# Three more column pairs of the up projection in the form with 42 products, with the buffers that this takes

## The chip, the cores and the metric

The kernel runs on one core of one Trainium2 chip. The metric is the device time of one execution in microseconds (us). The time before is 1391.71 us, the median of 3 runs (1391.12 to 1394.36). The profiled execution took 1392.02 us, and its span from the first to the last instruction is 1390.1 us.

## The reference, cut to what matters

One decoder layer over 256 tokens, all in float32. A mixing part (two branches, a gated delta rule and block attention) takes about half of the time and is not touched. What is touched is the first matmul of the MLP, `h @ w_up`:

```python
h = rms_norm(x, ln2[l])                                     # 256 x 2048
u = causal_dwconv(h @ w_up[l], ffn_conv[l], ffn_conv_bias[l])   # w_up: 2048 x 11264
u_gate, u_val = jnp.split(u, 2, axis=-1)                    # 5632 each
x = x + (jax.nn.silu(u_gate) * u_val) @ w_down[l]
```

## The kernel before

**Precision.** TensorE multiplies in fp32r. Each float32 operand is therefore split into a high part, `wh`, which is a cast on ScalarE (`split`, L104 and L105), and a low part, `wl`, which is the rest, a subtraction on VectorE (`low`, L101 and L102). A product of two operands is three matmuls: high by high, high by low, low by high. I call one such matmul of 128x512 a product step, or just a product, as the title counts them; 48 and 42 are numbers of these matmuls.

**Tiling.** The up projection is cut into 11 column pairs, `c` = 0 to 10 (loop at L1102). A pair has two sides of 512 columns each, side 0 for the gate and side 1 for the value, and two halves of 128 tokens, so four PSUM banks. D_MODEL is cut into 16 K-blocks of 128 rows. One fetch (`fetch`, L115) brings four K-blocks of one side, a quarter, as four DMAs of 256 KB each, issued on the POOL queue, into a buffer `wraw` of which there are four in rotation. A quarter has two raw halves; each is split once and then used by 12 matmuls, so a quarter takes 24 matmuls and a pair 8 x 24 = 192. `wh` and `wl` are rings of four slots: the cast for a part waits until TensorE has used up the part four places earlier.

**The shorter form.** For `c` in `UPS` (L30; before: 1 to 6) the first quarters of both sides are done together by `fewer` (L1028). The host interleaves their rows so that the four raw halves `r10`, `r11`, `r20`, `r21` are the four blocks of a 2x2 by 2x2 block product, done with seven block products for eight. That is 42 matmuls for 48, and it costs additions on VectorE: three before the first products (`t1 = r10 + r11`, `r11 += r21`, `t2 = t1 + r21`, all 128x1024), a fourth later (`t2 += r20`), four on PSUM banks (128x512), two copies on ScalarE, and seven splits where the two quarters need four. Six of the seven block products come first, then side 0's other three quarters (72 matmuls), then the function `rest` adds two banks and does the seventh block product with `r21`, then side 1's other three quarters.

**Buffers of the shorter form.** The first raw block `(r10, r11)` is an ordinary fetch. The second, `(r20, r21)`, is fetched during the pair before (L1113) into rows of `acts` that hold no results yet, `spare(28, 8)`. `acts` (44 rows of 256 columns) takes the activations; pair `c` fills rows 4c to 4c+3. `t1` is `acts` rows 24 to 27, `t2` rows 36 to 39, the fold sums rows 40 to 43. So the form could not be used for pairs whose results fill those rows. The weights fetched ahead into `acts` do not use up a `wraw` buffer.

**Order.** The program is written in the order of the loops; a scheduler then orders the instructions of each engine. Behind the matmuls run generators (`bg`), advanced once every 8 matmuls or so (`main_mm`, L93) except while `paused` is set, which `fewer` does: the convolutions of the results (`convolved`, L968; per side one 128x1024 transpose `xt<-ut` and eight or twelve short VectorE operations) and the transposition of the residual (`residual_turned`, L953; four transposes `xt<-x`, each followed by 16 small DMAs). A finished side is moved from PSUM into `ut` (L1082), of which there are two buffers.

## Time and profile before

| | |
|---|---|
| median of 3 runs | 1391.71 us (1391.12 to 1394.36) |
| the profiled execution | 1392.02 us |
| its span | 1390.1 us |
| granted TensorE clock | 0.999 |
| TensorE matmuls busy | 1378.3 us, 7186 matmuls |
| VectorE busy | 1096.4 us |
| ScalarE busy | 815.6 us |
| up projection, first to last matmul | 696.6 to 1157.3 us |
| its matmuls | 2076 |

The rows are from one profiled execution. The span lies inside the execution's own time; 1.9 us lie around it, and the median of the runs is 0.3 us under that time. Engines are PE (TensorE), DVE (VectorE), ACT (ScalarE), POOL (GpSimd, here a DMA queue). In a row of the timeline stand the start, the duration, the engine, the line, the operation, out<-in, the shape, the count, and in brackets the idle time before it with what ended it. A matmul's duration of 0.38 us overlaps with the next one's, so its cost in a stream is the distance between two starts.

### The profile page before, as it was taken

Reading aid. Unit: us, or ns where it says so; the run is one execution under the profiler, and the core shown is the slowest. Engines: PE = TensorE matmul, PEld = TensorE weight load, DVE = VectorE, ACT = ScalarE, POOL = GpSimd, SP = SyncE. Lnnn points to the kernel's source line nnn. Section 1 sums busy time; section 2 is a strip of 40 time slices with the busy share of each in tenths; the row PEclk is TensorE's granted clock in tenths of the full one; section 3 lists DMA queues with packets and bytes.
Section 4 is the critical chain, followed back from the end, with each engine's and each line's share of the span. In section 5 each row is a group of like instructions: output and inputs, shape, how many; then the busy total and the mean of one; then the engine's idle time right before and its main releaser. Section 6 shows DMA issues by size and latency. Waiting matters only on the chain.

```text
span 1390.1 us, 20248 instructions
## 1 busy us (share of the span) xinstructions
PE 1378.3 (99%) x7186; PEld 1194.9 (86%) x7186; DVE 1096.4 (79%) x1616; ACT 815.6 (59%) x1023; POOL 244.8 (18%) x424
## 2 busy tenths in 40 slices
PE   9999999999999999999999999999999999999997
PEld 8998899888888888889988888888888888888886
DVE  7988886977665446777668999999876777999995
ACT  6766545645466544445556676676665566676763
POOL 0021000200001100001344434434444320000000
PEclk9999999999999999999999999999999999999999
DMA  9566653567545565686567889898898976656561
GB/s 369 180 207 221 211 203 130 170 205 277 184 145 203 198 209 191 206 277 252 189 190 222 229 233 236 209 254 217 244 235 223 240 218 232 233 192 237 179 245 66
DMA packets 220165, 297.46 MB, mean 214 GB/s; under 512 B 171320, under 2 KB 173760, under 8 KB 198816
## 3 DMA queue, kind: packets, MB, share of 16 engines
q1 hardware_dynamic: 171984, 196.45, 44.3%
q0 software_dynamic: 30240, 96.04, 22.0%
q10 hardware_dynamic: 17840, 3.67, 1.4%
q8 instruction: 56, 0.92, 0.3%
q14 instruction: 45, 0.37, 0.1%
HBM read 273.48 MB, written 3.15 MB: 199 GB/s over the span
## 4 chain that ended last, share of the span: by engine, by line
PE 93%; DMA 4%; DVE 2%; SPq 1%; issue 0%; ACT 0%; DVEq 0%
PE ps_up L94 33%; PE pd L94 16%; PE ps_gate L94 12%; PE ps_gdn L94 9%; PE ps_wo L94 6%; PE ps_br L94 6%; PE ps_v L94 3%; PE ps_z L94 3%; PE ps_moba L94 2%; DMA wraw<-in_w_moba 2%; SPq L481 1%; DVE wl L102 1%; DMA xv<-xv 1%; PE ps_gdn L268 1%; DMA xs<-in_xw 0%; DMA dT<-X 0%
## 5 line engine op out<-in xcount | busy, mean ns | idle before, releaser
L102 DVE TENSOR_TENSOR wl<-wraw,wh 128x1024 fp32r<-128x1024 f32 (+1 forms) x464 | 557.9, 1211 | 208.1 <-ACT wh L105 204.8
L105 ACT CAST wh<-wraw 128x1024 fp32r<-128x1024 f32 (+1 forms) x464 | 477.6, 1038 | 411.2 <-PE ps_up L94 103.2
L94 PE MATMUL ps_up<-wh,h 128*128 128x512 f32 x1288 | 378.8, 380 | 0.2 <-DVE x L924 0.2
L94 PEld LDWEIGHTS ps_up<-wh,h 128*128 128x128 f32 x1288 | 241.5, 188 | 42.2 <-issue 0.6
L94 PE MATMUL ps_up<-wl,h 128*128 128x512 f32 x644 | 237.9, 381 | 1.2 <-DVE wl L102 1.0
L120 POOL DMA_DIRECT2D wraw<-in_w_up x328 | 174.5, 538 | 250.7 <-DVE wl L102 241.4
L94 PE MATMUL ps_gate<-wh,hc 128*128 128x512 f32 x512 | 155.4, 382 | 0.0
L94 PEld LDWEIGHTS ps_up<-wl,h 128*128 128x128 f32 x644 | 120.9, 188 | 24.3 <-DVE wl L102 3.7
L94 PE MATMUL ps_gdn<-hc,wh 128*128 128x256 f32 x720 | 124.2, 276 | 0.0
L94 PEld LDWEIGHTS ps_gate<-wh,hc 128*128 128x128 f32 x512 | 95.8, 188 | 16.3
L94 PEld LDWEIGHTS ps_gdn<-hc,wh 128*128 128x128 f32 x720 | 108.4, 188 | 1.3 <-issue 0.6
L94 PE MATMUL ps_gate<-wl,hc 128*128 128x512 f32 x256 | 98.0, 383 | 0.0
L94 PE MATMUL ps_gdn<-hc,wl 128*128 128x256 f32 x360 | 97.9, 275 | 0.0
L94 PE MATMUL ps_wo<-mc,wh 128*128 128x512 f32 x256 | 85.6, 379 | 0.0
L94 PE MATMUL pd<-tt,ah 128*128 128x512 f32 x282 | 82.0, 380 | 0.0
L94 PE MATMUL ps_moba<-wh,hc 128*128 128x512 f32 x256 | 77.1, 381 | 0.0
L94 PE MATMUL ps_wo<-mc,wl 128*128 128x256 f32 x256 | 70.5, 276 | 0.0
L105 ACT CAST tt<-wraw 128x1024 fp32r<-128x1024 f32 x46 | 47.1, 1044 | 36.3 <-PE pd L94 24.7
L94 PEld LDWEIGHTS ps_gdn<-hc,wl 128*128 128x128 f32 x360 | 67.1, 188 | 0.3
L94 PEld LDWEIGHTS pd<-tt,ah 128*128 128x128 f32 x282 | 52.9, 188 | 9.1
L94 PE MATMUL pd<-wh,ah 128*128 128x512 f32 x156 | 59.1, 380 | 0.0
L94 PE MATMUL pd<-wl,ah 128*128 128x512 f32 x156 | 59.1, 380 | 0.0
(465 smaller groups left out, 2177.1 us busy)
## 6 DMA issues: line engine op xcount, KB each, us to landing
wraw<-in_w_up POOLq DMA_DIRECT2D x328, 256.0 KB, 4.6
wraw<-in_w_dn SPq DMA_DIRECT2D x44, 1024.0 KB, 6.5
wraw<-in_w_gate SPq DMA_DIRECT2D x32, 1024.0 KB, 5.0
wraw<-in_w_gdn SPq DMA_DIRECT2D x22, 1024.0 KB, 4.9
wraw<-in_w_moba SPq DMA_DIRECT2D x16, 1024.0 KB, 6.2
wraw<-in_w_o SPq DMA_DIRECT2D x16, 1024.0 KB, 5.4
uc<-xt SPq DMA_DIRECT2D x352, 32.0 KB, 5.1
wraw<-in_w_z SPq DMA_DIRECT2D x8, 1024.0 KB, 6.9
```

The source lines that it names most:

```text
L94: r = pe.matmul(ps, a, b, start=start, stop=stop, skip_group_check=True)
L102: return (eng or dve).tensor_tensor(lo, src, hi.bitcast(F32), op=ALU.subtract)
L105: casts.append(act.copy(hi, src))
L120: fetcher[0].dma_start(raw[:, 512 * q:512 * q + 512], src[q])
L268: pe.matmul(ps_q0[:, b], wq[:, j, b * P:(b + 1) * P], xs[:, j], start=(j == b == 0), stop=False, skip_group_check=True)
L481: eng.dma_start(dst[32 * e:32 * e + 32, :, 32 * a:32 * a + 32], xt[32 * a:32 * a + 32, :, 32 * e:32 * e + 32])
```

## The change

`UPS` becomes 1 to 9, so that pairs 7, 8 and 9 take the shorter form too; the host's layout and the ring's first slot follow from `UPS`. The buffers are moved to make room. The fold sums get tiles of their own (`fold`, `fold2`), paid for with the second buffer of `ut`. The second raw block goes to `acts` rows 32 to 39, `t2` to rows 40 to 43, `t1` to rows 28 to 31. In pairs 8 and 9 rows 28 to 31 are taken, so `t1` is written over `r10`, and for that `r10` is split before the additions. In pair 9, the tenth, rows 32 to 39 are taken too, so its second raw block is fetched into an ordinary `wraw` buffer when the pair begins.

```diff
-UPS = (1, 2, 3, 4, 5, 6)
+UPS = (1, 2, 3, 4, 5, 6, 7, 8, 9)
...
-    def fewer(ps, raw1, raw2):
+    def fewer(c, ps, raw1, raw2):
         c11, c12, c21, c22 = ps
-        fold_v, fold_y = spare(40, 2), spare(42, 2)
+        fold_v = ub.tile([P, 512], F32, name="fold")
+        fold_y = ub.tile([P, 512], F32, name="fold2")
...
         (r10, r11), (r20, r21) = raw1, raw2
-        t1 = spare(24, 4)
-        t2 = spare(36, 4)
+        t1 = spare(28, 4) if c < 8 else r10
+        t2 = spare(40, 4)
+        w = part(r10) if c > 7 else None
         add(t1, r10, r11)
         add(r11, r11, r21)
         add(t2, t1, r21)
-        pair_of(c11, of(0, 0), part(r10), True)
+        pair_of(c11, of(0, 0), w or part(r10), True)
...
-        ut = ub.tile([P, 4, 2, P], F32, name="ut", bufs=2)
+        ut = ub.tile([P, 4, 2, P], F32, name="ut")
...
-            rest = fewer(ps, fetch(w_up[8 * c]), second)
+            first = fetch(w_up[8 * c])
+            rest = fewer(c, ps, first, second or fetch(w_up[8 * c + 4]))
...
-            second = fetch(w_up[8 * c + 12], spare(28, 8))
+            second = fetch(w_up[8 * c + 12], spare(32, 8)) if c < 8 else None
```

The order of the instructions moves with it. Two engines and three places matter.

VectorE, second half of pair 6, behind the splits of side 1's second quarter. Before, as there was no shorter pair behind it (`sgt` is the convolution of the gate side, `wraw_8534` the third quarter of side 1, `x1` the residual):

```order
L964 SCALAR_TENSOR_TENSOR sgt_8453<-uc_8113,ffv_5500,sgt_8453 128x255 x3
L964 SCALAR_TENSOR_TENSOR sgt_8453<-uc_8113,ffv_5500,sgt_8453 128x254
L964 SCALAR_TENSOR_TENSOR sgt_8453<-uc_8113,ffv_5500,sgt_8453 128x255
L964 SCALAR_TENSOR_TENSOR sgt_8453<-uc_8113,ffv_5500,sgt_8453 128x254 x3
L102 TENSOR_TENSOR wl_62<-wraw_8534,wh_61 128x1024
L476 STREAM_TRANSPOSE xt_8476<-ut_8460 128x1024
L476 STREAM_TRANSPOSE xt_8510<-x1_5499 128x1024
L102 TENSOR_TENSOR wl_62<-wraw_8534,wh_61 128x1024
```

The same place now (`wraw_8634` is the first raw block of pair 7, `wraw_8550` the third quarter of side 1 of pair 6):

```order
L1042 TENSOR_TENSOR acts_6142<-wraw_8634 128x1024
L964 SCALAR_TENSOR_TENSOR sgt_8465<-uc_8123,ffv_5500,sgt_8465 128x255
L964 SCALAR_TENSOR_TENSOR sgt_8465<-uc_8123,ffv_5500,sgt_8465 128x254
L964 SCALAR_TENSOR_TENSOR sgt_8465<-uc_8123,ffv_5500,sgt_8465 128x255
L964 SCALAR_TENSOR_TENSOR sgt_8465<-uc_8123,ffv_5500,sgt_8465 128x254
L1042 TENSOR_TENSOR wraw_8634<-wraw_8634,acts_6142 128x1024
L1042 TENSOR_TENSOR acts_6142<-acts_6142 128x1024
L102 TENSOR_TENSOR wl_62<-wraw_8550,wh_61 128x1024
L964 SCALAR_TENSOR_TENSOR sgt_8465<-uc_8123,ffv_5500,sgt_8465 128x254
L476 STREAM_TRANSPOSE xt_8488<-ut_8472 128x1024
L476 STREAM_TRANSPOSE xt_8526<-x1_5499 128x1024
L964 SCALAR_TENSOR_TENSOR sgt_8465<-uc_8123,ffv_5500,sgt_8465 128x254
```

The three additions for pair 7 have come in ahead of the split of the third quarter's first half; its second half's split is the next row.

POOL, the fetches of pair 9 in the order of issue, before (eight quarters, side 0 first):

```order
L120 DMA wraw_9342<-in_w_up 128x512 x4
L120 DMA wraw_9387<-in_w_up 128x512 x4
L120 DMA wraw_9433<-in_w_up 128x512 x4
L120 DMA wraw_9476<-in_w_up 128x512 x4
L120 DMA wraw_9514<-in_w_up 128x512 x4
L120 DMA wraw_9559<-in_w_up 128x512 x4
L120 DMA wraw_9606<-in_w_up 128x512 x4
L120 DMA wraw_9655<-in_w_up 128x512 x4
```

The same fetches now (`wraw_9358` holds `r10` and `r11`, `wraw_9363` holds `r20` and `r21`, then come side 0's other three quarters and side 1's, of which `wraw_9587` is the first):

```order
L120 DMA wraw_9358<-in_w_up 128x512 x4
L120 DMA wraw_9363<-in_w_up 128x512 x4
L120 DMA wraw_9427<-in_w_up 128x512 x4
L120 DMA wraw_9477<-in_w_up 128x512 x4
L120 DMA wraw_9528<-in_w_up 128x512 x4
L120 DMA wraw_9587<-in_w_up 128x512 x4
L120 DMA wraw_9640<-in_w_up 128x512 x4
L120 DMA wraw_9678<-in_w_up 128x512 x4
```

The count is the same, eight; the second block has moved from the fifth place to the second, and in a rotation of four buffers `wraw_9587`, four fetches later, gets its buffer.

VectorE, middle of pair 9, where side 1 begins. Before (`wraw_9476` is the last quarter of side 0, `wraw_9514` the first of side 1):

```order
L102 TENSOR_TENSOR wl_62<-wraw_9433,wh_61 128x1024
L964 SCALAR_TENSOR_TENSOR sgt_9428<-uc_9173,ffv_5500,sgt_9428 128x255 x2
L964 SCALAR_TENSOR_TENSOR sgt_9428<-uc_9173,ffv_5500,sgt_9428 128x254 x2
L102 TENSOR_TENSOR wl_62<-wraw_9476,wh_61 128x1024 x2
L102 TENSOR_TENSOR wl_62<-wraw_9514,wh_61 128x1024 x2
```

The same place now:

```order
L102 TENSOR_TENSOR wl_62<-wraw_9528,wh_61 128x1024
L476 STREAM_TRANSPOSE xt_9540<-x1_5499 128x1024
L981 TENSOR_TENSOR acts_6142<-sgt_9194,cvf_9449 128x256
L981 TENSOR_TENSOR acts_6142<-sgt_9194,cvf_9465 128x256
L102 TENSOR_TENSOR wl_62<-wraw_9528,wh_61 128x1024
L1042 TENSOR_TENSOR ps_up_9357<-ps_up_9357,fold_9368 128x512
L102 TENSOR_TENSOR wl_62<-wraw_9363,wh_61 128x1024
L964 SCALAR_TENSOR_TENSOR cvf_9490<-uc_9089,ffv_5500,cvf_9490 128x255
L1042 TENSOR_TENSOR ps_up_9355<-ps_up_9357,fold2_9369 128x512
L102 TENSOR_TENSOR wl_62<-wraw_9587,wh_61 128x1024
```

The last transpose of the residual, which stood in pair 8, has moved here, and the split of `r21` (`wraw_9363`) stands one row and one fold ahead of the first split of side 1.

## The prediction

> **What bounds the kernel now.** The page first: busy shares and the chain that ended last.
>
> ```profile
> PE 1378.3 (99%) x7186; PEld 1194.9 (86%) x7186; DVE 1096.4 (79%) x1616; ACT 815.6 (59%) x1023; POOL 244.8 (18%) x424
> PE ps_up L94 33%; PE pd L94 16%; PE ps_gate L94 12%; PE ps_gdn L94 9%; PE ps_wo L94 6%; PE ps_br L94 6%; PE ps_v L94 3%; PE ps_z L94 3%; PE ps_moba L94 2%; DMA wraw<-in_w_moba 2%; SPq L481 1%; DVE wl L102 1%; DMA xv<-xv 1%; PE ps_gdn L268 1%; DMA xs<-in_xw 0%; DMA dT<-X 0%
> ```
>
> The chain is almost wholly matmuls, a third of it the up projection. So a matmul less is worth its place in the stream, and a wait of TensorE costs what it lasts. Next the stretches of the column pairs, 1 to 9 in rows (the first six have 186 matmuls, the others 192; a stretch's count differs by one or two from where it was cut).
>
> ```profile
> core 0: us, PE busy (x) PEld busy (x) DVE busy (x) ACT busy (x) POOL busy (x), PEclk, DMA share, GB/s
> 739.90:780.90 41.00, 41.00 (x187) 34.84 (x186) 37.05 (x42) 27.55 (x32) 16.84 (x32) 1.00 0.75 211
> 780.90:822.00 41.10, 41.10 (x188) 34.84 (x187) 38.75 (x49) 27.08 (x34) 16.90 (x33) 1.00 0.90 230
> 822.00:863.50 41.50, 41.37 (x188) 34.76 (x187) 39.59 (x50) 27.04 (x34) 16.09 (x31) 1.00 0.88 231
> 863.50:906.30 42.80, 41.68 (x187) 34.68 (x186) 39.74 (x51) 27.63 (x35) 17.76 (x35) 1.00 0.86 229
> 906.30:947.50 41.20, 41.20 (x187) 34.84 (x186) 39.01 (x50) 27.38 (x35) 16.49 (x31) 1.00 0.87 233
> 947.50:988.40 40.90, 40.90 (x187) 34.92 (x186) 38.86 (x53) 29.27 (x38) 15.95 (x30) 1.00 0.89 230
> 988.40:1030.70 42.30, 42.30 (x194) 36.07 (x193) 30.86 (x43) 24.34 (x31) 17.02 (x32) 1.00 0.93 244
> 1030.70:1072.90 42.20, 42.20 (x193) 36.01 (x192) 30.29 (x39) 24.54 (x30) 17.00 (x32) 1.00 0.88 229
> 1072.90:1115.20 42.30, 42.30 (x194) 36.09 (x193) 29.42 (x38) 25.43 (x31) 17.00 (x32) 1.00 0.86 229
> ```
>
> Two things are in it. TensorE fills every pair, but VectorE works 38.8 to 39.7 us of 41 in a shorter pair (95%) and 29.4 to 30.9 of 42.2 in an ordinary one. And the shorter pairs aren't all equally short: pair 4 took 42.8 us, more than an ordinary one. Its loss can be seen on TensorE and, ahead of it, on VectorE:
>
> ```profile
> 896.09 0.49 PE L94 MATMUL ps_up<-wl,h 128*128 128x512 f32 x1 [1.00 <-DVE wl L102]
> ```
>
> ```profile
> 889.82 1.23 DVE L1041 TENSOR_TENSOR acts<-wraw 128x1024 f32<-128x1024 f32 x1 [1.53 <-DMA wraw<-in_w_up]
> 894.81 1.22 DVE L102 TENSOR_TENSOR wl<-wraw,wh 128x1024 fp32r<-128x1024 f32 x1
> ```
>
> The additions for pair 5 (L1041) stand in VectorE's queue ahead of a split that pair 4 still needs; the first of them waited 1.53 us for its weights, and the split came too late. VectorE is nearly the second bound here, and a DMA that it waits for becomes TensorE's wait.
>
> **What is removed.** Two consecutive matmuls, at the start of pair 6's seventh block product:
>
> ```profile
> 971.27 0.38 PE L94 MATMUL ps_up<-wh,ah 128*128 128x512 f32 x1
> 971.49 0.38 PE L94 MATMUL ps_up<-wh,al 128*128 128x512 f32 x1
> ```
>
> They start 0.22 us apart. 186 x 0.22 = 40.92 and 192 x 0.22 = 42.24, as pairs 6 and 8 show, so a pair saves 6 x 0.22 = 1.32 us and three pairs save 18 x 0.22 = 3.96 us: term A, -3.96. It is a ceiling, 0.28% of the time, just under the 0.3% that a measurement of this kernel can tell from no change.
>
> **What is added, and what hides it.** Per pair: three splits, four additions of 128x1024 and four of 128x512 on VectorE, three casts and two copies on ScalarE. The fetches stay eight a pair. ScalarE has 24 to 25 us of work in 42 and would have about 29, as pair 6 has: nothing. VectorE's load becomes that of pairs 2 to 6, 95%; it hides behind the matmuls as long as nothing makes VectorE wait, and where something does, TensorE pays as in pair 4. Three places must be looked at.
>
> *Second half of pair 6 (term B).* The three additions for pair 7 now come in here. The rows of before, with the fetch of what was pair 7's first quarter:
>
> ```profile
> 969.74 1.22 DVE L102 TENSOR_TENSOR wl<-wraw,wh 128x1024 fp32r<-128x1024 f32 x1
> 970.88 3.24 DVE L964 SCALAR_TENSOR_TENSOR sgt<-uc,ffv,sgt 128x255 f32<-128x255 f32 x8
> 974.03 1.22 DVE L102 TENSOR_TENSOR wl<-wraw,wh 128x1024 fp32r<-128x1024 f32 x1
> 975.16 1.24 DVE L476 STREAM_TRANSPOSE xt<-ut 128x1024 f32<-128x1024 f32 x1
> 976.33 1.21 DVE L476 STREAM_TRANSPOSE xt<-x 128x1024 f32<-128x1024 f32 x1
> 977.45 2.32 DVE L102 TENSOR_TENSOR wl<-wraw,wh 128x1024 fp32r<-128x1024 f32 x2
> ```
>
> ```profile
> 965.52 2.12 POOL L120 DMA_DIRECT2D wraw<-in_w_up x4 [1.60 <-DVE wl L102]
> ```
>
> Operations of 128x1024 follow each other every 1.14 us (969.74 to 970.88). The third quarter's second half is split from 977.45 to 978.6. TensorE wants it with the third matmul of its stretch: 971.27, and 6 + 24 + 12 + 2 matmuls of 0.22 on, 980.95. Spare: 2.35 us. Three additions take 3 x 1.14 = 3.4 us, so 1.1 us are lost even when the weights are there in time; their last piece is issued at 967.1, and VectorE comes to them at 971.7 (969.74, a split and two short operations of 0.4), about when a median landing (4.7 us, below) brings them. With pair 4's wait of 1.53 it is 2.6 us; if the scheduler's rows ran somewhat earlier it could be nothing. Pair 4 lost 42.80 - 40.92 = 1.9 in all. I take +1.5, ends 0 and 2.6.
>
> *The starts of pairs 7, 8 and 9 (term C).* In pairs 8 and 9 the additions stand behind the split of `r10`. That takes the additions out of the second halves of pairs 7 and 8, so term B does not come again, but it makes a chain: cast and split of `r10`, three additions, cast and split of `r11`. A cast and its split, on ScalarE and on VectorE:
>
> ```profile
> 985.76 1.05 ACT L105 CAST wh<-wraw 128x1024 fp32r<-128x1024 f32 x1 [1.09 <-PE ps_up L94]
> ```
>
> ```profile
> 986.85 1.23 DVE L102 TENSOR_TENSOR wl<-wraw,wh 128x1024 fp32r<-128x1024 f32 x1 [0.29 <-ACT wh L105]
> ```
>
> From the cast's start to the split's end 2.3 us. The ring lets `r10` be cast 36 matmuls ahead, 7.9 us before the pair begins: split done 5.6 before, additions done 2.2 before, `r11` split 0.1 after, and TensorE wants it 8 matmuls in, 1.76 after. 1.7 us to spare, more than the 1.53 that a late DMA took, since the weights of these pairs are asked for no earlier but wanted later. So I leave pairs 7, 8 and 9 the 0.1 us each that pairs 1 and 2 lost (41.0 and 41.1 against 40.92): +0.3. If VectorE comes to the chain over 1.7 us late, up to 2 us more in all.
>
> *The middle of pair 9 (term D).* The second raw block now lies in one of four `wraw` buffers, and the fourth fetch after it, side 1's first, must wait on POOL until `r21` is split; behind it on POOL wait side 1's other quarters and those of pair 10. In pairs 1 to 6 that quarter was fetched long before, and what waited for `r21` was the next pair's block in `acts`. When is `r21` split, and how soon does POOL follow? In pair 6, and in pair 1 with POOL's row:
>
> ```profile
> 965.75 0.47 DVE L964 SCALAR_TENSOR_TENSOR cvf<-uc,ffv,cvf 128x255 f32<-128x255 f32 x1
> 966.14 1.22 DVE L102 TENSOR_TENSOR wl<-acts,wh 128x1024 fp32r<-128x1024 f32 x1
> ```
>
> ```profile
> 758.11 1.22 DVE L102 TENSOR_TENSOR wl<-acts,wh 128x1024 fp32r<-128x1024 f32 x1
> ```
>
> ```profile
> 759.62 1.07 POOL L120 DMA_DIRECT2D acts<-in_w_up x2 [0.82 <-DVE wl L102]
> ```
>
> The landing of such a fetch, over the whole projection (first row) and in one lone group of four at 1007 us (second):
>
> ```profile
> DMA to landing us min/median/max: 2.8/4.7/7.7
> ```
>
> ```profile
> DMA to landing us min/median/max: 3.7/4.1/4.5
> ```
>
> Call R the start of the seventh block product (971.27 in pair 6). There `r21`'s split ended at 967.36, R - 3.9. In pair 9 one short operation (0.39) is no longer ahead of it and a residual transpose (1.14) is: R - 3.15. POOL starts 0.29 later (759.33 to 759.62), and the half that is wanted first is complete with the second of four DMAs, 0.53 on: issued at R - 2.3. The group is a lone one, so I take 4.1 us: landed R + 1.8, cast and split 2.3 more, R + 4.1. TensorE wants it 8 matmuls after R, R + 1.76. So +2.3 us. With a landing of 2.8 it is 1.0, with 7.7 it is 5.9; and if `r21` is split as early as it was in pair 1 (its end, 759.33, with R 108 matmuls after 739.9 at 763.7: R - 4.4) with a quick landing, it is nothing. Ends 0 and 5.9. The second half and the next quarters are then ahead again.
>
> The Trainium skill prices this fetch lower: "DMA: Bandwidth & Descriptors", section "Anatomy of one DMA — SWDGE (gpsimd) path", gives about 2.0 us plus the bytes over 436 GB/s, which for 256 KB is an estimate of 2.6 us. By it term D would be 0.8 us and the sum 1.5 us lower. This trace disagrees, with no landing under 2.8 us and a median of 4.7.
>
> *What costs nothing.* One `ut` buffer for two: a side's eviction must now wait for the transpose of the side before. In pair 6 that transpose ran at 975.16, and the next eviction here:
>
> ```profile
> 987.30 0.69 ACT L1085 ACTIVATE ut<-ps_up,R2c 128x512 f32<-128x512 f32 x1 [0.49 <-PE ps_up L94]
> ```
>
> 11 us of cover; if VectorE were later than that, a PSUM bank would come free late, by as much. The new places of `fold`, `t1`, `t2` change addresses alone, and their last readers are a pair away. The second blocks of pairs 7 and 8 are asked for on POOL in the pair before, as for pairs 2 to 6. The generators pause about six more times a pair, so the residual's last transpose comes a pair later; its place in pair 9 is in term D, and nobody waits for its 16 DMAs until the second half of the down projection.
>
> **The sum.** -3.96 + 1.5 + 0.3 + 2.3 = +0.1 us against the profiled execution's 1392.02, so 1392.2. The median of the runs stands 0.3 under that execution, so the median should be 1391.71 + 0.1 = 1391.9 (the sum unrounded is +0.14). A check from the stretches alone: pairs 1 to 6 took 41.42 on average, pairs 7 to 9 42.27, so 3 x 0.85 = 2.55 saved with the usual losses, and term D takes nearly all of it: -0.25.
>
> **The rivals.**
>
> *The gain is kept.* TensorE stays the only bound, as pairs 1, 2 and 6 show it, each within 0.2 of 40.92; the lone fetch lands in under 3 us and pair 6 has no loss. Then -3.96 + 0.3 = -3.7: 1388.0. For it: four of six pairs lost 0.3 or less. Against it: in pair 9 a prefetch of several us is gone for certain, and pair 6 has a residual transpose in the very place where three additions come in.
>
> *VectorE becomes the bound, slower.* At 95% a pair leaves it 2 us; additions that wait for weights use that up, and the backlog runs from pair to pair. The price is pair 4's: 1.9 us in each of pairs 7 to 9 as well as in pair 6, and with the backlog `r21` is split later too, so term D goes to about 4.5. -3.96 + 4 x 1.9 + 4.5 = +8.1: 1399.8. It decides from a loss of 8.2 us in all, of which term A gives 3.96 back and 4.2, 0.3% of the time, are left. For it: pairs 3, 4 and 5 all lost something. Against it: no pair's loss was carried into the next, pair 5 after the bad one needing only 41.2, and the additions of pairs 8 and 9 no longer stand ahead of splits that the pair before still needs.
>
> **How the numbers follow.** The forecast, a wash between -2.5 and +3: 0.65. The gain kept: 0.22. VectorE bound: 0.13. Likeliest time 1391.9. The range goes down to just under the kept gain, 1387.9, and up to where B and D both stand near their upper ends with C as forecast (-3.96 + 2.6 + 0.3 + 4.4 = +3.3), 1395.0; it leaves out the slower rival, 0.13, and little else. Faster by over 0.3% needs the whole of term A and something more, such as losses of pairs 3 to 5 that don't come again: 0.05. Slower by over 0.3%: 0.11, nearly all of it the slower rival's. Within 0.3%: 0.84.
>
> **What would show it.** Right: 2058 matmuls of `ps_up`; pairs 7 and 8 of about 41.0 us; an idle stretch of TensorE of 1 to 2 us late in pair 6, released by VectorE's `wl`; another of about 2 us at the beginning of side 1 in pair 9, with POOL's fetch held until `r21` is split and ScalarE's cast waiting for a DMA. The first wrong step would be term D if side 1 of pair 9 begins without a wait, term B if pair 6 still takes 40.9, term C if pair 8 begins with an idle TensorE while VectorE does additions. The forecast as a whole is wrong if a loss appears outside pairs 6 to 9, in the down projection above all, where the change moves single rows only.

## The result, and the profile after

The changed kernel took **1400.72 us** (median; 1395.73 to 1409.05), the kernel before 1392.55 (1391.12 to 1394.36) in the same rounds: 1.0065 times as long, 95% interval 1.0043 to 1.0087. That is 8.2 us slower, where 0.2 us slower was forecast and the range ended at 1395.0. The profiled execution of the changed kernel (1395.73 us, span 1393.5) is the fastest of its runs. A second one, from the experiments, took 1401.67 (span 1399.4) and shows a typical run.

The page of the changed kernel, busy shares and the chain, and the chain of the kernel before:

```profile
PE 1377.0 (99%) x7168; PEld 1191.1 (85%) x7168; DVE 1127.0 (81%) x1649; ACT 823.8 (59%) x1038; POOL 244.5 (18%) x424
PE 88%; DVE 5%; DMA 4%; issue 2%; SPq 1%; ACT 0%; DVEq 0%; ACTq 0%
```

```profile
PE 93%; DMA 4%; DVE 2%; SPq 1%; issue 0%; ACT 0%; DVEq 0%
```

The 18 matmuls are gone (7186 to 7168; 2058 of `ps_up`). But TensorE's share of the chain fell from 93% to 88%, and VectorE's rose from 2% to 5%; the DMAs' is 4% in both. The stretches of pairs 4 to 9, cut where a pair's first matmul starts:

```profile
core 0: us, PE busy (x) PEld busy (x) DVE busy (x) ACT busy (x) POOL busy (x), PEclk, DMA share, GB/s
861.64:904.98 43.34, 41.70 (x188) 34.68 (x187) 39.76 (x51) 27.65 (x35) 17.75 (x35) 1.00 0.87 227
904.98:946.94 41.96, 41.52 (x188) 34.75 (x187) 39.11 (x50) 27.38 (x35) 16.44 (x31) 1.00 0.87 230
946.94:990.96 44.02, 42.12 (x187) 34.60 (x186) 40.13 (x51) 27.40 (x35) 17.09 (x33) 1.00 0.81 218
990.96:1031.88 40.92, 40.92 (x187) 34.91 (x186) 38.42 (x49) 27.04 (x35) 15.85 (x30) 1.00 0.95 250
1031.88:1073.11 41.23, 41.22 (x188) 34.83 (x186) 40.03 (x51) 27.71 (x35) 14.87 (x28) 1.00 0.84 216
1073.11:1117.08 43.97, 41.21 (x187) 34.83 (x186) 36.68 (x50) 28.49 (x36) 17.00 (x32) 1.00 0.72 201
```

Pair 7 is as short as its matmuls allow (186 x 0.22 = 40.92), pair 8 nearly so. Pairs 6 and 9 lose 3.1 us each. From here on a pair's **gap** is its time less its matmuls at 0.22 us. (In the table it is summed over the steps from one matmul to the next that are plainly longer; steps longer by a hundredth or two are left out, so that it can fall short of the full time by up to 0.25 us.) Pair 6 on VectorE, and TensorE's wait:

```profile
973.77 1.23 DVE L1042 TENSOR_TENSOR acts<-wraw 128x1024 f32<-128x1024 f32 x1 [1.05 <-DMA wraw<-in_w_up]
...
980.32 1.24 DVE L476 STREAM_TRANSPOSE xt<-ut 128x1024 f32<-128x1024 f32 x1
981.48 1.20 DVE L476 STREAM_TRANSPOSE xt<-x 128x1024 f32<-128x1024 f32 x1
982.61 0.44 DVE L964 SCALAR_TENSOR_TENSOR sgt<-uc,ffv,sgt 128x254 f32<-128x254 f32 x1
982.96 3.49 DVE L102 TENSOR_TENSOR wl<-wraw,wh 128x1024 fp32r<-128x1024 f32 x3
```

```profile
980.06 0.49 PE L94 MATMUL ps_up<-wl,h 128*128 128x512 f32 x1 [1.20 <-DVE wl L102]
```

The additions (L1042), the side's transpose and the residual's (`xt<-x`) all stand ahead of splits that TensorE needs. Pair 9 is another matter; its transposes on VectorE, then TensorE:

```profile
1081.95 1.23 DVE L476 STREAM_TRANSPOSE xt<-ut 128x1024 f32<-128x1024 f32 x1
...
1088.05 1.24 DVE L476 STREAM_TRANSPOSE xt<-x 128x1024 f32<-128x1024 f32 x1
...
1105.55 1.25 DVE L476 STREAM_TRANSPOSE xt<-ut 128x1024 f32<-128x1024 f32 x1 [6.00 <-DMA uc<-xt]
```

```profile
1109.92 0.49 PE L94 MATMUL ps_up<-wl,h 128*128 128x512 f32 x1 [2.76 <-DVE wl L102]
```

TensorE did not wait where side 1 begins (from 1096.87 on, term D's place), but 10 us later. VectorE had stood idle for 6.00 us ahead of a transpose that waited for DMAs out of an `xt` buffer, with the splits behind it in its queue. The typical execution shows the same, longer:

```profile
1083.50 1.24 DVE L476 STREAM_TRANSPOSE xt<-ut 128x1024 f32<-128x1024 f32 x1
...
1089.61 1.24 DVE L476 STREAM_TRANSPOSE xt<-x 128x1024 f32<-128x1024 f32 x1
...
1108.56 1.25 DVE L476 STREAM_TRANSPOSE xt<-ut 128x1024 f32<-128x1024 f32 x1 [7.52 <-DMA x<-xt]
```

```profile
1108.30:1113.00 4.70, 0.42 (x3) 0.06 (x1) 4.44 (x8) 0.60 (x1) 0.00 (x0) 0.80 0.14 21
1113.00:1118.20 5.20, 5.20 (x13) 4.09 (x14) 5.20 (x9) 3.56 (x4) 4.08 (x8) 0.53 0.79 222
```

TensorE stood for 4.5 us, and then the granted clock was 0.53 for 5.2 us, in which 13 matmuls started in place of 23: another 2.3 us lost.

Against before's 1390.1 us of span, the typical execution's 1399.4 adds up so: the matmuls -3.96, pair 9 +6.99, pair 6 +3.81, pair 8 +0.54, pairs 1 to 5 +0.5 (3.34 for 2.85), what follows the up projection +1.9, its start -0.5 (696.15 for 696.63): +9.3.

### The profile page after: what moved, and what is told of

The parts are those of the page before. It is cut to its first block, busy times and chain, and to the rows that moved or that the text cites. A ratio compares the mean times of both kernels' runs of the same rounds, so it can differ in the third digit from the quotient of the medians.

```text
span 1393.5 us, 20278 instructions
## 1 busy us (share of the span) xinstructions
PE 1377.0 (99%) x7168; PEld 1191.1 (85%) x7168; DVE 1127.0 (81%) x1649; ACT 823.8 (59%) x1038; POOL 244.5 (18%) x424
## 4 chain that ended last, share of the span: by engine, by line
PE 88%; DVE 5%; DMA 4%; issue 2%; SPq 1%; ACT 0%; DVEq 0%; ACTq 0%
PE ps_up L94 28%; PE ps_gate L94 12%; PE pd L94 11%; PE ps_gdn L94 9%; PE ps_wo L94 6%; PE ps_moba L94 6%; PE ps_br L94 6%; PE ps_v L94 3%; PE ps_z L94 3%; DMA uc<-xt 2%; DVE wl L102 2%; DMA wraw<-in_w_dn 1%; DVE tt L102 1%; DVE wraw L1167 1%; SPq L481 1%
## 5 line engine op out<-in xcount | busy, mean ns | idle before, releaser
L105 ACT CAST wh<-wraw 128x1024 fp32r<-128x1024 f32 x462 | 474.6, 1038 | 390.0 <-PE ps_up L94 85.2
L102 DVE TENSOR_TENSOR wl<-wraw,wh 128x1024 fp32r<-128x1024 f32 x462 | 554.1, 1210 | 174.9 <-ACT wh L105 170.6
L94 PE MATMUL ps_up<-wh,h 128*128 128x512 f32 x1228 | 357.6, 381 | 0.3 <-DVE x L924 0.2
L94 PEld LDWEIGHTS ps_up<-wh,h 128*128 128x128 f32 x1228 | 230.1, 188 | 40.9 <-DVE ps_up L1042 0.7
L94 PE MATMUL ps_up<-wl,h 128*128 128x512 f32 x614 | 223.3, 382 | 6.8 <-DVE wl L102 6.5
L120 POOL DMA_DIRECT2D wraw<-in_w_up x320 | 170.0, 538 | 249.2 <-DVE wl L102 238.1
L94 PEld LDWEIGHTS ps_up<-wl,h 128*128 128x128 f32 x614 | 115.2, 188 | 31.2 <-DVE wl L102 11.6
L102 DVE TENSOR_TENSOR tt<-wraw,tt 128x1024 fp32r<-128x1024 f32 x46 | 55.2, 1217 | 6.2 <-ACT tt L105 6.0
```

Source lines behind the costliest of these rows:

```text
L94: r = pe.matmul(ps, a, b, start=start, stop=stop, skip_group_check=True)
L102: return (eng or dve).tensor_tensor(lo, src, hi.bitcast(F32), op=ALU.subtract)
L105: casts.append(act.copy(hi, src))
L120: fetcher[0].dma_start(raw[:, 512 * q:512 * q + 512], src[q])
```

## The experiments

Two theories of pair 9: the block `r21` in a fetch buffer holds POOL's fetches, which then come in a burst (theory 1), or the residual's fourth transpose, pushed into pair 9 by the longer pauses, stops VectorE (theory 3). Two of the rest: the additions ahead of the splits (theory 2, term B), or VectorE's load wherever they stand (theory 4). The table has every kernel that ran, with each profiled execution's gaps in us. Two more that were written did not fit into SBUF and have no time: pair 9's second block in `acts` with `t2` in a tile of its own, and the same with the late residual and the early split as well. "Behind" is the time from the last matmul of the up projection to the end, less before's 233.0.

| kernel | median us | ratio to before (95%) | pairs 1-5 | 6 | 7 and 8 | 9 | behind |
|---|---|---|---|---|---|---|---|
| before | 1392.55 | 1 | 2.85 | 0 | 0 | 0 | 0 |
| changed | 1400.72 | 1.0065 (1.0043-1.0087) | 4.16 | 3.06 | 0.30 | 3.05 | 1.4 |
| changed, again | 1402.70 | 1.0069 (1.0047-1.0091) | 3.34 | 3.81 | 0.54 | 6.99 | 1.9 |
| pair 9 ordinary | 1395.91 | 1.0020 (1.0008-1.0033) | 3.83 | 2.86 | 3.39 | 0 | 0.3 |
| buffers alone | 1393.15 | 0.9998 (0.9988-1.0007) | 5.84 | 0 | 0 | 0 | 0 |
| `r21` copied | 1404.45 | 1.0074 (1.0058-1.0090) | 7.44 | 2.68 | 0.96 | 5.10 | 4.2 |
| late residual | 1397.64 | 1.0045 (1.0030-1.0059) | 6.43 | 1.73 | 0.62 | 0 | 5.3 |
| `r10` split written first | 1400.16 | 1.0048 (1.0035-1.0061) | 3.34 | 2.56 | 3.22 | 1.83 | 12.7 |
| sooner residual | 1397.16 | 1.0036 (1.0022-1.0051) | 7.85 | 2.50 | 0.28 | 0 | 0 |
| additions held | 1406.34 | 1.0094 (1.0079-1.0109) | 5.70 | 0 | 7.43 | 5.69 | 3.6 |
| sooner and held | 1406.65 | 1.0104 (1.0081-1.0127) | 8.34 | 3.78 | 4.82 | 0 | 0 |
| before, held | 1393.00 | 1.0006 (0.9998-1.0015) | 6.39 | 0 | 0 | 0 | 0 |
| before, light | 1394.30 | 1.0011 (1.0001-1.0020) | 7.62 | 0.09 | 0 | 0 | 0 |
| changed, light | 1397.54 | 1.0045 (1.0027-1.0062) | 4.40 | 1.38 | 0.09 | 4.47 | 6.8 |
| first residual | 1392.02 | 0.9992 (0.9983-1.0002) | 7.65 | 0.60 | 0 | 0 | 0 |
| first and light | 1388.75 | 0.9976 (0.9965-0.9987) | 4.58 | 0.09 | 0.09 | 0 | 0 |
| first residual, SP | 1397.89 | 1.0039 (1.0024-1.0054) | 12.9 | 0.10 | 0 | 0 | 0 |
| before, the same | 1401.28 | 1.0058 (1.0044-1.0073) | 16.6 | 0 | 0 | 0 | 0 |
| residual on SP | 1406.45 | 1.0088 (1.0065-1.0111) | 11.1 | 1.80 | 3.09 | 4.67 | 0.5 |
| residual in pair 0 | 1395.82 | 1.0029 (1.0010-1.0048) | 8.77 | 1.23 | 0 | 0 | 0.2 |

**Where the loss is.** The changed kernel again, without an edit.

> The changed kernel once more, for a second profile of it. The profiled execution after the change took 1395.73 us, the median of its runs 1400.72: some 5 us of the loss are in no profile yet. If the loss is one of a chain with fixed parts (additions ahead of splits in pair 6, 3.06 us of gaps; the late transpose in pair 9, 3.05 us), this profile shows the same two gaps at the same places, 2.5 to 4 us each, and the rest is lost where transfers happen to land late. If VectorE is the bound all over, the gaps of pairs 1 to 9 grow together, each by 0.5 us or more. Median 1398 to 1403, +0.4 to +0.75% against before.

It is the typical execution above: the same two gaps, 3.81 us and 6.99, the second larger than expected; the clock was halved behind both stalls.

```diff
-UPS = (1, 2, 3, 4, 5, 6, 7, 8, 9)
+UPS = (1, 2, 3, 4, 5, 6, 7, 8)
```

> Pairs 1 to 8 in the short form, pair 9 in the ordinary one: the held fetches of the middle of pair 9 are gone, and 6 matmuls of 0.22 us are back (+1.32). Theory 1, the middle of pair 9 carries the loss (r21 in a fetch buffer holds POOL's fetches, these come in a burst, and what follows is late): 1400.7 + 1.3 - 3.05 = 1399.0 from the gap of the one profile, and 1393 to 1396 if the unexplained 5 us of the other runs are lost there too. Theory 2, the additions that come into pair 6 and VectorE's load carry it: 1400.7 + 1.3 = 1402, no better than the changed kernel. Against before: theory 1 +0.1 to +0.45%, theory 2 +0.6 to +0.75%.

1395.9: with 6 matmuls more it is 5 to 7 us faster. Pair 9 carries most of the loss, pair 6 (2.86 us) and the starts of pair 8 the rest.

```diff
-UPS = (1, 2, 3, 4, 5, 6, 7, 8, 9)
+UPS = (1, 2, 3, 4, 5, 6)
```

> Pairs 1 to 6 as before, with the new buffers alone: one ut for two, fold tiles of their own, t1, t2 and the second raw block at other places. If the buffers cost nothing, as predicted, it is 1392.5, within 0.15% of before. If the single ut holds a side's eviction back behind VectorE's transpose (a bank late by a few tenths of a us per side, 22 sides), it is 1394 to 1400, and the gap would show as TensorE waiting for ScalarE's ut.

No difference: the single `ut` and the fold tiles cost nothing, as predicted.

**Is it the held fetch buffer?** `r21` is copied away early in pair 9, so that its buffer comes free some 8 us before the split.

```diff
+        if c > 8:
+            act.copy(t2, r21)
+            r21 = t2
```

> The changed kernel with one more copy on ScalarE in pair 9 alone: r21 is copied to t2, whose last reader is done, so its fetch buffer comes free some 8 us before its split, and side 1's fetches go out one by one and earlier. Theory 1, the held fetches and their burst carry the loss of pair 9: its gap goes from 3.05 us to under 1, the time is 3 us or more under the changed kernel's in the same rounds (1397 or less; 1393 if the other runs' loss is there too). Theory 2, the loss is VectorE's load and the additions in pair 6: within 1 us of the changed kernel, 1400. The residual's transpose holding an xt buffer in pair 9 (theory 3) would leave most of the gap too, but then VectorE still waits ahead of its transpose for the DMAs of xt.

No better: 1404.5, and pair 9's gap is 5.10. But the copy could not have helped the first fetch of side 1, for `r21` had not held it. That fetch is the sixth of pair 9, and in the first profile POOL issued it 9.2 us into the pair; `r21` was split 9.3 us later:

```profile
1082.32 2.12 POOL L120 DMA_DIRECT2D wraw<-in_w_up  x4 [3.91 <-DVE wl L102]
```

```profile
1091.59 1.21 DVE L102 TENSOR_TENSOR wl<-wraw,wh 128x1024 fp32r<-128x1024 f32 x1
```

In the built program that fetch has the address of side 0's second quarter, and the one that follows `r21` into its buffer is the first of pair 10. With the copy it takes the buffer of `r21`, and was issued 9.8 us into the pair (1087.39). So theory 1 falls as it was put, by its first half; whether the burst of fetches alone does the harm is left to the next run. ScalarE now stood where VectorE had stood; its row, and the row in its queue ahead of it:

```profile
1105.98 0.62 ACTq L481 DMA_DIRECT2D x<-xt  x1
1106.78 1.04 ACT L105 CAST wh<-wraw 128x1024 fp32r<-128x1024 f32 x1 [6.96 <-PE ps_up L94]
```

It had done nothing since 1099.83 but issue this DMA, one of the residual's. In the built program that DMA has to wait for one of the side's on SP's queue, with which it shares a semaphore; it was issued at 1092.48 and landed 13.5 us later.

**Is it the residual?** Its fourth transpose is put off into pair 10, and nothing else changed.

```diff
         for q_ in range(4):
+            yield from wait(22 * (q_ // 3))
```

> The changed kernel with the residual's fourth transpose and its 16 DMAs put off by 22 steps of the generators, out of pair 9 into pair 10. Theory 3: in pair 9 that transpose holds one of the two xt buffers, and its DMAs on ScalarE's queue share their semaphores with those on SP, so a held-up transfer stops VectorE or ScalarE; without it pair 9's gap (3.05, 6.99 and 5.10 us in three profiles) falls under 1.5 us and the time is 1394 to 1397. Theory 1, the burst of held fetches alone does it: the small transfers still land late, VectorE or TensorE still waits in pair 9, gap 2.5 us or more, 1399 to 1402.

Pair 9's gap is 0. VectorE's transposes in the same stretch:

```profile
1083.27 1.23 DVE L476 STREAM_TRANSPOSE xt<-ut 128x1024 f32<-128x1024 f32 x1
...
1102.09 1.23 DVE L476 STREAM_TRANSPOSE xt<-ut 128x1024 f32<-128x1024 f32 x1
```

No wait ahead of the second one, although POOL's fetches came in a like burst (12 pieces of 256 KB from 1087.83 to 1096, for 1086.51 to 1095.6 in the first profile). So theory 3 holds: without a residual in pair 9 the burst does no harm. But 5.3 us are lost later: the residual's last DMA was issued at 1209.8, in the down projection. Then the residual the other way, sooner:

```diff
-            yield from turn(..., act, 1, 3)
+            yield from turn(..., act, 1, 2)
```

> The changed kernel with the residual's DMAs issued every third step of the generators instead of every fourth, so that all four of its transposes and their 64 DMAs are done before pair 9, as they were before the change. The late residual (put off into pair 10) took pair 9's gap to 0 but left 5.2 us of waits in the down projection, where its last DMAs had been pushed. Theory 3, a residual that is late collides first with the up projection's transposes and then with the down projection's weights: here both are gone, pair 9's gap under 0.5 us, the down projection 233 us as before, 1394 to 1396 in all. If the down projection's waits come from the changed pairs themselves (fewer buffers ahead at its start), it stays at 234 us or more, and the time is 1397 or more.

Pairs 1 and 9 of it:

```profile
738.90:781.92 43.02, 41.59 (x187) 34.69 (x186) 36.90 (x42) 27.36 (x33) 16.03 (x31) 1.00 0.70 196
...
1077.05:1117.97 40.92, 40.92 (x187) 34.91 (x186) 39.38 (x56) 29.96 (x39) 19.10 (x36) 1.00 0.85 234
```

Pair 9 at 40.92 and 0 behind, as theory 3 has it. The time is still 1397: pairs 1 and 2 lose 3.7 us, where they lost 0.4 in the changed kernel. Which way does a late residual act? Its DMAs on SP's queue in place of ScalarE's:

```diff
-            yield from turn(..., act, 1, 3)
+            yield from turn(..., sp, 1, 3)
```

> The changed kernel with the residual's DMAs on SP's queue instead of ScalarE's, at the same steps. If ScalarE's queue is the way (a DMA that it can't issue yet holds the casts behind it), pair 9's gap falls under 1.5 us and the down projection's waits go: 1395 to 1397. If it is the xt buffer and the small transfers that land late, pair 9's gap stays at 3 to 7 us and the time at 1399 to 1403.

```profile
1091.58 1.24 DVE L476 STREAM_TRANSPOSE xt<-ut 128x1024 f32<-128x1024 f32 x1
1097.70 1.24 DVE L476 STREAM_TRANSPOSE xt<-x 128x1024 f32<-128x1024 f32 x1
1114.34 1.25 DVE L476 STREAM_TRANSPOSE xt<-ut 128x1024 f32<-128x1024 f32 x1 [5.56 <-DMA x<-xt]
```

The same picture, so ScalarE's queue is not needed for it. What is left is the buffer. There are two `xt` buffers, and a turn of the residual holds one of them from its transpose to the landing of its last DMA (in the changed kernel the fourth from 1088.05 to 1162.3 and later); the sides' transposes then have one and the same address in the built program, and each must wait until the 16 DMAs of the side before have landed. In the built program the waiting transpose waits for exactly these 16, and it starts 0.1 to 0.2 us after the last of them has landed (1105.4, 1108.4 and 1114.2 in the first, the typical and this profile). In the changed kernel and in the one before the sides share one address almost throughout, since one residual turn follows the other; what counts is whether the 16 DMAs are done when VectorE comes. In pair 9 of the first profile VectorE was ready for the next transpose 17.6 us after the last (1099.55 for 1081.95), and the buffer was free after 23.6 (1105.55); in the two other profiles above it was 25.1 and 22.8. The late and the sooner residual leave both buffers to the sides there. The kernel before has the same wait, in pair 7, where an ordinary pair leaves VectorE time enough to hide it:

```profile
994.15 1.25 DVE L476 STREAM_TRANSPOSE xt<-ut 128x1024 f32<-128x1024 f32 x1 [2.95 <-DMA x<-xt]
```

That a residual in pair 9 is the cause is shown; that it acts through the buffer is read from these rows and the built program. No run gave the sides a second buffer with the residual in place: the kernel with a tile of its own for `t2` left 42.1 KB a partition for a pool that takes 44, and a third `xt` buffer is as large as that tile. Why the DMAs took 23 to 25 us there and some 19 in other pairs (975.16 to 994.15) is open. The burst alone is not enough: beside a like burst in the late and the sooner residual, with no residual DMAs among them, the last of the 16 landed 20.0 and 19.8 us after the transpose (1103.2 and 1105.7). At 20.0 the wait in the first profile would have been 2.4 us (20.0 - 17.6, an estimate) and not 6.0.

**Term B: additions ahead of splits.** First the split of `r10` was written ahead of the additions in all pairs.

```diff
-        w = part(r10) if c > 7 else None
+        w = part(r10)
```

> The changed kernel with the split of r10 ahead of the three additions in all pairs, not only in the last two, so that no addition stands ahead of a split that the pair before still needs. Term B's theory: the gaps late in pairs 2 to 6 (0.2, 0.4, 2.1, 1.0 and 3.0 us in the first profile) go, and 0.1 to 0.5 us come at the start of pairs 2 to 7: 4 to 6 us less than the changed kernel, 1395 to 1397. Pair 9's theory: the loss of pair 9 stays, 3 to 7 us. If VectorE's load is what binds (theory 4), the waits only move to the starts of the pairs, and the time stays within 1.5 us of the changed kernel's.

VectorE's queue had the additions in the same place in pairs 1 to 6, and pair 6 kept 2.56 us. (This profile is of a 1409.05 execution; see the last section.) Then they were held by an order:

```diff
+        w = part(r10)
+        with tc.issue_after(lows[-1].ins):
+            add(t1, r10, r11)
+            add(r11, r11, r21)
+            add(t2, t1, r21)
```

> The changed kernel with the three additions held, in every pair, until the split of r10 has been issued on VectorE (the early kernel only changed the order in which they are written, and VectorE's queue still had them ahead of the splits of the pair before). Term B's theory: the gaps late in pairs 4, 5 and 6 (2.4, 1.0 and 3.1 us) fall under 0.5 each, at 0.1 to 0.5 us for each pair's start: 4 to 6 us less than the changed kernel, 1395 to 1397. Theory 4, VectorE's load binds: the waits move to the starts of pairs 2 to 9, 1 to 2.6 us each, as pair 8 of the early kernel had it, and the time is 1399 or more.

Pair 6's gap is gone, and 5.6 us slower for it: pairs 7 to 9 lose 13 us, at their starts and late in their second halves. The same with the sooner residual, and on the kernel before:

> The sooner residual and the held additions together. If term B and the late residual are the loss, and nothing else, 18 matmuls fewer are left: before 1392.4 - 3.96 - 2.7 (gaps of pairs 3 to 5 that before has too) + 0.1 to 0.5 for each of nine starts: 1387 to 1390, 0.2 to 0.4% faster than before. If VectorE's load binds, 1393 or more.

> The kernel before (six short pairs) with the additions held until the split of r10 is issued. If the additions ahead of the splits cost pairs 3 to 5 their 2.7 us, 1389.5 to 1390.5, 0.15 to 0.2% faster. If the waits move to the starts, 1392 or more.

1406.7 and 1393.0. The waits move, and neither place that was tried for the additions is better than where they were: theory 2 falls as a cure.

**VectorE's load.** One of the two shifted taps of each convolution is left out (part of the computation is missing, so only the times count).

```diff
-        for d in (1, 2):
+        for d in (1,):
```

> The kernel before, with one of the two additions of a shifted tap left out of each convolution of the up projection, so that VectorE has 8 operations of about 0.39 us less a pair, 3.1 of some 39 us. It is the reference for the two kernels below. If VectorE's load makes the gaps of pairs 3 to 5 (0.6, 1.9 and 0.3 us), they fall under 0.3 together: 1389.5 to 1390.5. If they come from the places of single operations and from late weights, they stay: 1392 to 1393.

> The changed kernel with the same taps left out. If VectorE's load binds in pairs 1 to 6, their gaps (7 us in two profiles) fall under 2, and pair 9 keeps its own loss only as far as the residual's late DMAs make it: 1389 to 1396, with a gap of more than 2 us in pair 9 and a wait in the down projection, if VectorE has to wait there for DMAs; under 1 us in pair 9, if the load is behind that too. If places bind, 1399 to 1401.

On the changed kernel the gaps of pairs 2 to 5 fall to 1.0 in all and pair 6's to 1.4, but pair 9 keeps 4.47: there VectorE waits for DMAs, whatever its load. On the kernel before it was no gain, since pairs 1 to 3 lost 6.9, and VectorE, being earlier, waited longer for `xt` buffers: 15.7 us in all by these two rows, for 3.9 in the kernel before.

```profile
DVE xt L476 <- DMA x<-xt: 10.7, 3, 4.6
...
DVE xt L476 <- DMA uc<-xt: 5.0, 3, 4.1
```

Now the residual from pair 0 on, without and with the taps left out:

```diff
-        yield from wait(26)
+        yield from wait(4)
...
-            yield from turn(..., act, 1, 3)
+            yield from turn(..., act, 1, 1)
```

> The changed kernel with the residual's four transposes and 64 DMAs as early as they can be, from pair 0 on and every second step of the generators. Pair 9's gap and the down projection's waits should be gone as with the sooner residual (0 and 0). If a residual transpose costs a short pair some 1.5 us wherever it stands on a VectorE that is full, the pairs 1 and 2 lose 0 to 2 us, since VectorE has the convolutions of fewer sides in them, and pairs 4 to 6 lose 1 us less than with the sooner residual: 1393 to 1395.5. If the place is indifferent, 1397 as with the sooner one.

> The early residual and the left-out taps together on the changed kernel. If VectorE's load and the residual's place are the whole loss, what is left of the change is its 18 matmuls: light_before less 3.5 to 4 us, 1385.5 to 1387. If single places and late weights cost the new short pairs their gain in any case, it stays within 1.5 us of light_before.

1392.0 with the whole computation: 8.7 us less than the changed kernel from moving four transposes and 64 small DMAs, and level with before. Pairs 7 to 9 have no gap, pair 6 has 0.6, nothing is lost behind; pairs 1 to 3 pay 5.0. With the taps left out 1388.75; its pair 4:

```profile
865.72:906.75 41.03, 41.03 (x188) 34.84 (x186) 36.16 (x42) 27.93 (x35) 17.00 (x32) 1.00 0.82 233
```

At 36.2 us of VectorE work in 41 the gaps of pairs 4 to 9 are at most 0.1 each; at 39 to 40 those of pairs 4 to 6 are up to 4.3 and change from run to run. Theory 4 holds for pairs 4 to 6, but not alone: with the residual in it pair 6 kept 1.4 us with the taps left out.

**What the 18 matmuls are worth.** The residual on SP's queue in pairs 0 and 1, on both kernels:

```diff
-        yield from wait(26)
+        yield from wait(4)
...
-            yield from turn(..., act, 1, 3)
+            yield from turn(..., sp, 2, 1)
```

> The changed kernel with the residual's 64 DMAs on SP's queue, two for every second step of the generators, from pair 0 on, so that all four transposes are done within pairs 0 and 1, where VectorE has few convolutions. The early residual on ScalarE's queue left gaps of 1.1, 2.7 and 1.2 us in pairs 1 to 3 and took 1392.0. If a residual transpose costs only where VectorE is full, pairs 1 to 3 go back to about 0.8 in all and the time is 1392.0 - 4.2 = 1388, 0.2 to 0.4% faster than before. If the transfers themselves disturb whatever pair they lie in, 1391 to 1393.

> The kernel before with the same residual: what the 18 matmuls are worth is the difference to it. If VectorE's load alone makes the gaps of pairs 3 to 5, it gains little, 1391.5 to 1392.5, and the changed kernel with the early residual is 2 to 4 us under it. If the residual was behind the gap of 1.9 us in pair 4 (a residual transpose stands at its start), 1389.5 to 1390.5, and the change is worth 0 to 2 us.

Both lose 7.6 to 8.2 us in pair 1, where residual and convolutions meet. From pair 6 on the residual is out of the way; pairs 6 to 9 of the changed kernel, then of before with the same residual:

```profile
956.89:997.93 41.04, 41.04 (x188) 34.84 (x186) 39.02 (x50) 27.38 (x35) 17.48 (x34) 1.00 0.84 232
997.93:1038.85 40.92, 40.92 (x188) 34.91 (x186) 39.08 (x50) 27.63 (x35) 15.40 (x30) 1.00 0.92 249
1038.85:1079.77 40.92, 40.92 (x188) 34.91 (x186) 39.32 (x50) 27.30 (x34) 14.86 (x28) 1.00 0.75 207
1079.77:1120.69 40.92, 40.92 (x188) 34.92 (x186) 39.27 (x56) 30.05 (x39) 19.12 (x36) 1.00 0.85 235
```

```profile
959.52:1000.44 40.92, 40.92 (x187) 34.92 (x186) 39.13 (x56) 29.37 (x39) 15.92 (x30) 1.00 0.87 228
1000.44:1042.68 42.24, 42.24 (x193) 36.04 (x192) 30.02 (x40) 24.28 (x30) 16.99 (x32) 1.00 0.83 229
1042.68:1084.92 42.24, 42.24 (x193) 36.04 (x192) 29.42 (x38) 24.37 (x30) 17.00 (x32) 1.00 0.79 229
1084.92:1127.16 42.24, 42.24 (x193) 36.04 (x192) 29.42 (x38) 25.36 (x31) 16.98 (x32) 1.00 0.79 224
```

163.80 us for 167.64: 3.84 of the 3.96 are kept, and the medians stand 3.4 apart (the two intervals against before overlap a little). A last try to get the residual out of everybody's way, all of it in pair 0:

```diff
-        yield from wait(26)
+        yield from wait(2)
...
-            yield from turn(..., act, 1, 3)
+            yield from turn(..., sp, 4, 1)
```

> The changed kernel with the residual's four turns at the convolutions' pace (four DMAs a step, SP's queue), from the second step of pair 0 on, 9 us each, so that the last xt buffer of the residual is free when the first convolution wants it. If the wait for an xt buffer is what a residual costs, pairs 1 to 3 go back to 0.8 us of gaps in all, pairs 4 to 6 keep 2 to 4, pairs 7 to 9 none: before 1392.7 - 3.96 + 0.5 to 1.5 against before's 2.9, 1389.2 to 1390.2. If the last residual turn still meets the first convolution's, 3 to 5 us are lost at the start of pair 1, as with the one before: 1393 to 1395.

1395.8, from 1388.2 to 1402.3: the fourth turn came at 751.6, in pair 1, which lost 5.6. No version with the whole computation was found that beats the kernel before by more than can be measured.

## Why the prediction was wrong, step by step

- **Term A** held: 2058 matmuls, 0.22 us apart, 40.92 us in pair 7, 3.84 of 3.96 kept where nothing interferes.
- **Term B** had the right place and mechanism and the wrong size: +1.5, with an upper end of 2.6, was 3.06 and 3.81 in the two profiles (1.73 to 2.86 in the six other kernels that have the changed pair 6 with its residual transpose, the additions where they were and all taps). The first addition's wait for its weights, 1.05 us, was within the bounds, but the working started VectorE on time, and it was late already: it was ready for that addition 25.8 us into the pair (972.72 - 946.94), where the prediction had 24.2 (971.7 - 947.5). Pair 6 without the residual (the first residual on SP), the same stretch:

```profile
981.46 1.23 DVE L1042 TENSOR_TENSOR acts<-wraw 128x1024 f32<-128x1024 f32 x1 [0.33 <-DMA wraw<-in_w_up]
...
987.98 1.24 DVE L476 STREAM_TRANSPOSE xt<-ut 128x1024 f32<-128x1024 f32 x1
989.14 0.44 DVE L964 SCALAR_TENSOR_TENSOR sgt<-uc,ffv,sgt 128x254 f32<-128x254 f32 x1
989.50 3.49 DVE L102 TENSOR_TENSOR wl<-wraw,wh 128x1024 fp32r<-128x1024 f32 x3
```

The last splits come 32.6 us into the pair there (989.50 - 956.89), and 36.0 in the changed kernel (982.96 - 946.94): 1.1 for the residual's transpose, 0.7 for the DMA, and the rest, 1.6, is that lateness. Earlier in the pair VectorE had waited for an `xt` buffer here too, 1.5 us longer than in the kernel before (0.80 at 957.22) and not at all in the first residual on SP, so the lateness is most likely of the same origin as pair 9's loss:

```profile
958.20 1.25 DVE L476 STREAM_TRANSPOSE xt<-ut 128x1024 f32<-128x1024 f32 x1 [2.34 <-DMA x<-xt]
```

With the residual elsewhere pair 6's gap is 0.1 to 1.2. The additions alone nearly fit; with a residual transpose as well they don't.
- **Term C** held: +0.3 was 0, 0.3 and (at pair 9's start) 0.
- **Term D** named a wait that isn't there, and its premise was wrong. It took the buffer of `r21` for that of the fourth fetch after it, as the section on the change does (`wraw_9587`). The program gives that fetch a buffer that came free earlier: it was issued at 1082.32, 9.3 us before `r21` was split. The late and the sooner residual had pair 9 at 40.92. The +2.3 should have been 0.
- **The step that failed** stands in "What costs nothing": the residual's last transpose comes a pair later, "and nobody waits for its 16 DMAs until the second half of the down projection". Nor does anybody wait for these 16. But until they have landed the residual holds one of two `xt` buffers; the sides' transposes share the other, which a short pair wants back after 17.6 us and got after 23.6, and one that waits for it stops VectorE with every split behind it. That cost 3.05 and 6.99 us in pair 9, where the prediction had another loss: that it expected a gap there was luck. It looked for readers of what the DMAs write, and not for who wants the buffer that they read. The row at 994.15 had it, in the trace of before.
- **Behind the up projection** nothing was forecast, and a loss there was named as what would make the whole wrong. It is 1.4 and 1.9 us. In the light changed kernel, where it is largest but for the execution with the slower matmuls (last section), ScalarE shows it:

```profile
1186.80 1.99 ACT L105 CAST tt<-wraw 128x1024 fp32r<-128x1024 f32 x2 [9.72 <-DMA wraw<-in_w_dn]
```

A weight of the down projection came late. All kernels whose residual had its last DMA issued by 1161 us lose at most 0.6 there, all those in which it was issued at 1162 or later (1162.3 in the changed kernel, 1168.3 in the typical execution, 1209.8 in the late residual) 1.4 and more. How it delays that fetch (SP has the weights behind the sides' 16 DMAs, which took 13.15 us for 11.21 before) is not settled.
- **The rivals.** "VectorE becomes the bound", at 1399.8, came within 1 us of the median, but only in part by its mechanism: VectorE's load costs pair 6, pairs 7 and 8 lose little, and pair 9's loss is a wait for a buffer.

## What to carry to other kernels

When a change moves a background task, ask for each of its instructions not only who reads the result but whose buffer it holds and for how long: where it takes one of two buffers for two pairs, the others must be done with the one that is left before they want it again, and VectorE, which runs its queue in order, stops there with all that stands behind. And check in the built program which buffer a fetch gets before a wait is built on it. On an engine that is 95% full, a price for three operations is not three operations less the spare: what else was put into the same stretch, and how late the engine comes to it, must be read from the pair that will have them. And a matmul saved is worth its time only where nothing else in its stretch is late; move the neighbour (here four transposes and 64 small DMAs, 8.7 us) before giving up the change.

## What the runs showed of the hardware

A stall of TensorE can cost more than it lasts, other than the prediction has it ("a wait of TensorE costs what it lasts"). In the typical execution a stall of 2.0 us in pair 6 was followed by 4.1 us with a granted clock of 0.58 and 11 matmuls in place of 18 or 19; in the profile of the fastest run one of 2.9 us in pair 9 was followed by none. First the wait and what came behind it in the one, then the stall of pair 9 in the other:

```profile
980.75 0.49 PE L94 MATMUL ps_up<-wl,h 128*128 128x512 f32 x1 [1.84 <-DVE wl L102]
```

```profile
980.70:984.80 4.10, 4.05 (x11) 3.24 (x12) 4.10 (x6) 1.20 (x2) 0.00 (x0) 0.58 0.11 16
```

```profile
1106.80:1109.90 3.10, 0.37 (x2) 0.00 (x0) 3.10 (x7) 0.00 (x0) 0.00 (x0) 1.00 0.21 32
1109.90:1114.30 4.40, 4.38 (x20) 3.75 (x21) 4.40 (x6) 3.44 (x4) 3.20 (x7) 1.00 0.68 204
```

The Trainium skill, "TensorE: Matmul & The Clock Gate", section "Part 1: The HAM clock gate (the "warmup" mystery)", has the half clock come after at least one idle window of about 3.4 us, and the windows run freely. Half clock and run-to-run chance agree with these rows. The length doesn't: 2.0 us of standing were enough here, and 2.9 not always. It may make part of the scatter of the slower kernels.

In the profiled execution of the kernel with `r10` written first (1409.05 us), the matmuls from 1240 us on stand 0.23 us apart, 174 in 40 us, where the changed kernel has 184. The granted clock reads 1.00 in both:

```profile
1240.00:1280.00 40.00, 40.00 (x174) 32.36 (x173) 38.81 (x52) 27.48 (x39) 0.00 (x0) 1.00 0.63 223
```

That is some 9 us of its 12.7 behind the up projection; the cause is open, and so is whether the changed kernel's own run of 1409.05 is the same.
